# Seven-product units whose second half is added by accumulating transfers, in a hybrid encoder layer on one core

## The chip, the core and the metric

The kernel runs on one core of a Trainium2 chip. Time is what the device takes for one execution, in microseconds (us). A core has TensorE (matmuls; PE in the profile, PEld for its weight loads), VectorE (DVE), ScalarE (ACT), GpSimd (POOL) and SyncE (SP, which here only issues transfers), each with its own queue of instructions that it runs in order. Matmuls write to PSUM, eight banks of 128 x 512 float32; all else is in SBUF or in the chip's main memory (HBM).

## What is computed

One layer is applied to two sequences, a sample of 1024 positions and a prompt of 512, with shared weights and 2048 features:

```python
h = rms_norm(x, norm_g)
z = h @ w_in                     # 2048 x 5632
c_val, c_glu, c_gate, q, k, v, a_gate = jnp.split(z, split_points, axis=-1)
...
conv_out = conformer_conv(c_val, c_glu, w_dw, b_dw, ln_g, ln_b, w_pw) * jax.nn.silu(c_gate)
attn_out = banded_sink_attention(q, k, v, sink) * jax.nn.silu(a_gate)
mix = jnp.concatenate([conv_out, attn_out], axis=-1) @ w_out
return x + mix
```

`conformer_conv` is `c_val * sigmoid(c_glu)`, a convolution of 31 taps in each channel, a layer norm, a silu and a product with `w_pw`. The attention is banded and has rotary positions on q and k. A final RMS norm follows. Everything is float32: each operand is split into a high and a low part, and a product is three matmuls (high-high, high-low, low-high).

## The kernel before

**Units.** The input projection of the sample is done by 44 units (`Unit`). A unit takes two blocks of 128 columns of `w_in`, half of the depth (1024 features, called g = 0 or 1) and all 1024 positions. It sees this as a product of 2 x 2 blocks, and makes it with seven block products instead of eight: `make0` to `make3` (L120 to L150) form the sums of weights on VectorE and split them into parts, `block_sums` (L549) does the like with the tokens. Each product is 4 x 3 = 12 matmuls of 512 columns (L179). The products go to three accumulating banks; after each, `tap` takes the bank's content into one of four results, named (0,0), (0,1), (1,1), (1,0) by half of the positions and column block. Results are complete after products 1, 4, 5 and 6, counted from 0.

**Four stages.** 8 convolution units at g = 0, the same 8 at g = 1, 14 others (gates, keys and values, queries) at g = 1, the same 14 at g = 0. So there are two kinds. A *half-depth* unit (the first and third stage) copies or adds its products into new tiles (`tap_part`: ScalarE copies at L213 for products 0, 2, 3, 6; VectorE adds at L220 for the rest) and stores the four results to HBM (`part`). A *finishing* unit (second and fourth stage) loads these four tiles back (`load_parts`, L159 to L164, on SyncE's queue), either when it opens or already after product 4 of the unit ahead of it, adds all seven products to them on VectorE (`tap_sum`, L205) and calls `done` on each complete result. In the second and fourth stage the first two units run side by side.

**What `done` does.** For a convolution unit (`gated`, L673): the gate's column is scaled (L681), goes through a sigmoid (L682) and is scaled again (L683); once both columns of one half are there, they are multiplied (L687) and stored. For the fourteen others: a query's or key's result is turned (`rope`, L748 to L751, on VectorE), a gate's or value's result is scaled (L696) and then goes through a silu (L701, ScalarE) or is transposed (`turn_value`).

**Tiles.** The results lie in tiles from `E()`, which hands out tiles of two pools of four by turns; silu, rope, and other code take tiles from the same pools. Prepared weights (`hl`) have three buffers, raw ones three.

**What sets the order.** The program is written down once, in Python, and a scheduler places each engine's instructions by priority and by when they can run, using estimates of its own. `urgently` and `high_priority(URGENT)` move code ahead by 400 places: weight preparation and `tap`, with `done` in it, are written so. Three lanes (`attn`, `conv`, `prep`) hold work that is fed in between: for each three matmuls `tick` credits a lane 3 x 216 = 648, times its rate, and a lane's work pays what it yields. The convolution taps (`taps`, L720) of the sample go through the `conv` lane. The mean squares (`rms_ahead`, L616 to L630) and then the scaling of the prompt's input (`scale_ahead`, L639 to L653) go through the `prep` lane at rate 1; the first ends with a reciprocal root (`rsqrt`, L486 to L491) and a yield, the second begins with `spread` (L493 to L506), which puts the 512 numbers on all partitions: small VectorE instructions (L498, L499, L504) and two matmuls with ones (L505), in whose result the scaling is done (L651).

**Signs.** The sums are written as additions only. One token sum (`s1`) and one of the two columns come out negative; the sign is taken back in `val`, in the taps' weights, in the silu's scale and in `turn_value`.

After the sample's units follow the prompt's projections and the products with `w_pw` and `w_out` as plain jobs (L439), attention among them, and a last pass (L1165).

Of the kernel before, what the change touches and what calls it, by code (L numbers as in the profile page):

```python
# [46 lines left out]

SUMS = ("A11", "A12", "S2", "s1", "S3", "S4", "A22")
BANK = (0, 1, 0, 2, 0, 2, 0)
# [32 lines left out]
class Unit:  # L82
# [37 lines left out]
    def make0(self):  # L120
# [6 lines left out]
        return t  # L127

    def make1(self):
        add = lambda o, x, y: self.e.nc.vector.tensor_tensor(o, x, y, ALU.add)  # L130
        self.t = self.raw()
        add(self.t[:, 0], self.r1[:, 0], self.r2[:, 0])
        add(self.t[:, 1], self.t[:, 0], self.r2[:, 1])
        t = self.e.hl_tile()
        self.e.parts(t[:, 0], t[:, 1], self.t)
        return t

    def make2(self):
        self.e.nc.vector.tensor_tensor(self.r2[:, 0], self.r2[:, 0], self.r2[:, 1], ALU.add)
        t = self.e.hl_tile()  # L140
        self.e.parts(t[:, 0], t[:, 1], self.r2)
        self.r2 = None
        return t

    def make3(self):
        self.e.nc.vector.tensor_tensor(self.r1[:, 1], self.r1[:, 1], self.t[:, 1], ALU.add)
# [51 lines left out]
    def tap(self, step):  # L198
        if self.done:
            self.tap_sum(step)  # L200
        else:
            self.tap_part(step)

    def tap_sum(self, step):
        add = lambda n, b: self.e.nc.vector.tensor_tensor(self.d[n], self.bank[b], self.d[n], ALU.add)  # L205
        n = ((0, 0), (0, 0), (0, 1), (1, 1), (1, 1), (0, 1), (1, 0))[step]
        add(n, (0, 1, 0, 2, 0, 2, 0)[step])
        if step in (1, 4, 5, 6):
            self.done(n[0], n[1], self.d.pop(n))

    def tap_part(self, step):
        e, nc = self.e, self.e.nc
        copy = lambda n, b: nc.scalar.activation(self.d[n], self.bank[b], AF.Copy)  # L213
        n = ((0, 0), (0, 0), (0, 1), (1, 1), (1, 1), (0, 1), (1, 0))[step]
        b = (0, 1, 0, 2, 0, 2, 0)[step]
        if step in (0, 2, 3, 6):
            self.d[n] = e.E()
            copy(n, b)
        else:
            nc.vector.tensor_tensor(self.d[n], self.bank[b], self.d[n], ALU.add)  # L220
        if step in (1, 4, 5, 6):
            e.store(self.part[n[0]][n[1]], self.d.pop(n))

# [34 lines left out]
class Encoder:  # L258
# [84 lines left out]
    def constants(self):  # L343
        nc, a = self.nc, self.a

        def load(key, shape):
            t = self.const.tile([P] + shape, F32, name="c_" + key)
            nc.sync.dma_start(t, a[key])
            return t

        self.norm_g = load("norm_g", [ND])
        self.norm_n = self.const.tile([P, ND], F32, name="norm_n")
        nc.vector.tensor_scalar(self.norm_n, self.norm_g, -1.0, None, ALU.mult)
        self.ones = self.const.tile([P, P], F32, name="ones")
        nc.vector.memset(self.ones, 1.0)
        self.ones_r = self.const.tile([P, P], F32R, name="ones_r")
        nc.vector.tensor_copy(self.ones_r, self.ones)

        def rest():
            self.ident = load("ident", [P])  # L360
            self.mask = load("mask", [3 * P])

            self.w_dw = load("w_dw", [NC, TAPS])
            nc.vector.tensor_scalar(self.w_dw, self.w_dw, -1.0, None, ALU.mult)
# [44 lines left out]
    def run(self, items):  # L409
# [3 lines left out]
        for n, item in enumerate(items):  # L413
# [3 lines left out]
            if isinstance(item[0], Unit):  # L417
                ahead = items[n + 1]
# [90 lines left out]
class Sequence:  # L509


    def __init__(self, e, s):
# [19 lines left out]
        if s == 1:  # L532
            self.xr_d = dram("xr_d", [2, self.T], ND // 2)
        else:
            self.h_d = dram("h_d", [self.T], NC)
            self.sums_d = {(g, n): dram(f"sum_{g}_{n}", [W], HALF) for g in (0, 1) for n in ("s1", "S2", "S3", "S4")}

# [11 lines left out]
    def block_sums(self, k0, k1, x0, x1):  # L549
# [8 lines left out]
        return {"s1": s1, "S2": s2, "S4": t, "S3": s3}  # L558

# [14 lines left out]
    def first_sums(self, x):  # L574
# [5 lines left out]
        for j in range(HALF):  # L580
            sums = self.block_sums(j, j + HALF, x[j], x[j + HALF])
            for name in ("S2", "s1", "S3", "S4"):
                self.token_sum(name, 0, j, sums[name])
                e.store(self.sums_d[0, name][j], sums[name])
# [16 lines left out]
    def load_sum(self, name, g):  # L601
        e = self.e
        out = []
        for j in range(HALF):
            x = e.PT("p", NP, [W])
            if name in ("s1", "S2", "S3", "S4"):
                src = self.sums_d[g, name][j]
# [8 lines left out]
    def rms_ahead(self):  # L616
# [12 lines left out]
        e.rsqrt(self.rcol, v, self.B)  # L629
        yield 500  # L630

# [65 lines left out]

    def silu_of(self, dst, sign):
# [64 lines left out]
    def value(self, g, accs):  # L763
        e = self.e
        z = e.G()
        e.nc.scalar.activation(z, accs[0], AF.Copy)
        e.prep.add(self.turn_value(g, 0, z, 1.0))

    def negative_value(self, g):
        def done(t, z):  # L770
            self.scaled(z, t)
            self.e.attn.add(self.turn_value(g, t, z, -1.0))

        return done

    def turn_value(self, g, c, z, sign):
# [5 lines left out]
        nc.scalar.activation(z, ps, AF.Copy, scale=sign)  # L782
        e.store(self.v_d[g][:, c * W : c * W + W], z)
# [96 lines left out]
    def units(self):  # L880

        e, w = self.e, self.e.a["w_in"]

        def both(cols, name, done):
# [8 lines left out]
        for i in range(0, NC, 2):  # L893
            done = each(self.silu_of(self.gate_d[i], 1.0), self.silu_of(self.gate_d[i + 1], -1.0))
            gates.append(both((GATE + i, GATE + i + 1), f"gate{i}", done))
        rest = gates[:2] + [
            both((K + g, V + g), f"kv{g}", each(self.rotate(self.k_d[g]), self.negative_value(g))) for g in range(2)
        ]
        for h in range(HEADS):
            turn = self.rotate(self.q_d[h // GROUP][:, h % GROUP])  # L900
            rest.append(both((Q + h, AG + h), f"q{h}", each(turn, self.silu_of(self.ag_d[h], -1.0))))
        return conv, rest + gates[2:]

    def jobs(self):
        e, w = self.e, self.e.a["w_in"]
        job = lambda c, evac, **kw: Job(w[c], list(range(ND)), self.T, self.rhs, evac, **kw)
        conv = lambda i: [
# [497 lines left out]
```

## Time and profile before

| | |
|---|---|
| median of 3 runs | 2232.35 us (2229.7 to 2236.6) |
| the profiled execution | 2230.47 us |
| its span in the profile | 2228.7 us |
| mean granted TensorE clock | 0.984 |
| the first, second, third and fourth stage of units | about 0 to 188, to 346, to 634, to 937 us |
| transfers issued by GpSimd | none |

A row of the timeline gives start, length, engine, line and operation, what is written and read by the program's names, how many were merged, and in brackets how long the engine stood idle before and what ended that. A row of the waits reads "who <- for whom: us in total, times, longest". In a row for stretches of time each engine's busy time stands with its instruction count, then the granted TensorE clock, the share of the DMA engines and GB/s.

These are the chain that ended last, by engine, and the whole span in 40 slices, in tenths of each slice:

```profile
PE 68%; DVE 17%; DMA 9%; issue 4%; ACT 3%; SPq 0%; ACTq 0%; DVEq 0%
```

```profile
PE   6999998899989999999999999999999999999998
DVE  8648999999999999999677879977673578446343
```

The chain runs through TensorE for two thirds; VectorE is at nine tenths or more from the fourth slice to the eighteenth, which are the second to the fourth stage.

### The profile page before, as it was taken

What the parts mean: (1) busy time and instruction counts of PE and PEld (TensorE: products, weight loads), DVE (VectorE), ACT (ScalarE), POOL (GpSimd) and SP (SyncE); (2) the same over time, 40 slices, a digit from 0 to 9 for tenths busy, and PEclk for the clock granted to TensorE, in tenths of its full rate; (3) what the DMA queues carried; (4) which work ended last, traced back from release to release, by engine and by line L of the source; (5) the groups of instructions that cost most, each with busy time, mean ns of one, the idle gap of its engine ahead of it and who ended that gap; (6) DMA issues with size and microseconds to landing.
All of it is one profiled execution on the core that took longest, in us unless ns stands there. A gap on an engine that the chain in (4) does not pass through costs nothing.

```text
span 2228.7 us, 26104 instructions
## 1 busy us (share of the span) xinstructions
PE 2144.1 (96%) x9510; PEld 1754.4 (79%) x9510; DVE 1732.5 (78%) x2608; ACT 927.5 (42%) x1400; POOL 0.2 (0%) x4
## 2 busy tenths in 40 slices
PE   6999998899989999999999999999999999999998
PEld 4877786688867887788888888887888778888886
DVE  8648999999999999999677879977673578446343
ACT  5455324233343222433345446654562446322232
POOL 0000000000000000000000000000000000000000
PEclk8999999899999999999999999999999999999999
DMA  8866644633365545733333533337543466527342
GB/s 285 308 202 224 216 128 165 217 129 128 132 232 170 165 142 179 242 127 121 125 113 110 168 106 117 109 119 251 170 151 109 137 213 209 171 102 264 95 133 76
DMA packets 195072, 365.48 MB, mean 164 GB/s; under 512 B 17536, under 2 KB 75264, under 8 KB 194944
## 3 DMA queue, kind: packets, MB, share of 16 engines
q1 hardware_dynamic: 194944, 363.82, 49.0%
q8 instruction: 74, 1.21, 0.2%
q14 instruction: 54, 0.44, 0.1%
HBM read 276.72 MB, written 87.03 MB: 163 GB/s over the span
## 4 chain that ended last, share of the span: by engine, by line
PE 68%; DVE 17%; DMA 9%; issue 4%; ACT 3%; SPq 0%; ACTq 0%; DVEq 0%
PE a L439 18%; PE a L179 10%; PE b L439 9%; PE c L439 9%; PE c L179 5%; DVE hl L333 3%; DVE f L720 3%; PE s L830 2%; PE b L179 2%; PE a L1165 2%; PE s L1165 2%; DMA u<-q_d 2%; PE pv L862 2%; DMA raw<-w_in 1%; PE pt L867 1%
## 5 line engine op out<-in xcount | busy, mean ns | idle before, releaser
L332 ACT ACTIVATE hl<-raw 128x1024 fp32r<-128x1024 f32 (+1 forms) x367 | 369.7, 1008 | 651.7 <-PE a L439 138.4
L333 DVE TENSOR_TENSOR hl<-raw,hl 128x1024 fp32r<-128x1024 f32 (+1 forms) x367 | 424.5, 1157 | 206.6 <-ACT hl L332 200.9
L179 PE MATMUL a<-t,hl 128*128 128x512 f32 x1968 | 487.4, 399 | 29.3 <-ACT t L335 8.5
L439 PE MATMUL a<-t,hl 128*128 128x512 f32 x2112 | 506.1, 391 | 0.0
L179 PEld LDWEIGHTS a<-t,hl 128*128 128x128 f32 x1968 | 376.7, 193 | 119.8 <-ACT t L335 8.9
L439 PEld LDWEIGHTS a<-t,hl 128*128 128x128 f32 x2112 | 393.3, 188 | 79.1
L720 DVE SCALAR_TENSOR_TENSOR f<-f,c_w_dw,f 128x1024 f32<-128x1024 f32 (+1 forms) x464 | 452.7, 1010 | 2.5 <-ACT f L715 2.4
L439 PE MATMUL b<-t,hl 128*128 128x512 f32 x1056 | 255.8, 393 | 4.4 <-ACT hl L332 2.5
L179 PE MATMUL c<-t,hl 128*128 128x512 f32 x984 | 243.8, 393 | 12.5 <-ACT t L332 7.7
L439 PE MATMUL c<-t,hl 128*128 128x512 f32 x1056 | 253.7, 392 | 0.0
L439 PEld LDWEIGHTS b<-t,hl 128*128 128x128 f32 x1056 | 196.3, 188 | 44.2 <-ACT hl L332 3.2
L179 PEld LDWEIGHTS c<-t,hl 128*128 128x128 f32 x984 | 185.7, 189 | 55.3 <-ACT t L332 9.4
L439 PEld LDWEIGHTS c<-t,hl 128*128 128x128 f32 x1056 | 197.0, 188 | 39.8
L179 PE MATMUL b<-t,hl 128*128 128x512 f32 x492 | 119.0, 389 | 0.0
L179 PEld LDWEIGHTS b<-t,hl 128*128 128x128 f32 x492 | 92.4, 188 | 19.2
L1165 PE MATMUL a<-hl,t 128*128 128x512 f32 x192 | 74.7, 390 | 0.0
L332 ACT ACTIVATE a<-pt 128x512 fp32r<-128x512 f32 x64 | 38.1, 595 | 86.4 <-PE pt L867 86.1
L830 PE MATMUL s<-t,a 128*128 128x384 f32 (+1 forms) x288 | 58.6, 329 | 9.9 <-ACT a L332 9.0
L130 DVE TENSOR_TENSOR raw<-raw,raw 128x512 f32<-128x512 f32 x82 | 56.1, 684 | 14.6 <-DMA raw<-w_in 12.3
L844 ACT ACTIVATE p<-p,tiny 128x384 f32<-128x384 f32 (+1 forms) x96 | 54.5, 570 | 29.3 <-DVE tiny L841 29.1
L333 DVE TENSOR_TENSOR a<-pt,a 128x512 fp32r<-128x512 f32 x64 | 44.0, 687 | 29.1 <-ACT a L332 28.9
L830 PEld LDWEIGHTS s<-t,a 128*128 128x128 f32 x288 | 47.8, 188 | 20.7 <-ACT a L332 13.2
(245 smaller groups left out, 2049.9 us busy)
## 6 DMA issues: line engine op xcount, KB each, us to landing
raw<-w_in SPq DMA_DIRECT2D x169, 512.0 KB, 4.0
raw<-w_out SPq DMA_DIRECT2D x64, 512.0 KB, 3.7
raw<-w_out SPq DMA_DIRECT2D x64, 256.0 KB, 3.3
raw<-w_pw SPq DMA_DIRECT2D x24, 512.0 KB, 3.6
f<-xT_s SPq DMA_DIRECT2D x38, 256.0 KB, 6.1
f<-x_s SPq DMA_DIRECT2D x16, 512.0 KB, 7.2
f<-x_p SPq DMA_DIRECT2D x13, 512.0 KB, 6.9
p<-xT_s SPq DMA_DIRECT2D x24, 256.0 KB, 3.6
```

The source lines that it names most:

```text
L130: add = lambda o, x, y: self.e.nc.vector.tensor_tensor(o, x, y, ALU.add)
L179: nc.tensor.matmul(acc, hl[:, l, o, j, :], toks[j][:, r], start=step in FRESH and j == 0 and q == 0, stop=step in LAST and j == HALF - 1 a ...
L332: nc.scalar.activation(hi, x, AF.Copy)
L333: nc.vector.tensor_tensor(lo, x, hi.bitcast(F32), ALU.subtract)
L439: nc.tensor.matmul(job.acc[0], hl[:, l, kk // HALF, kk % HALF, :], r, start=i == 0 and p == 0, stop=i == nk - 1 and p == 2,)
L720: nc.vector.scalar_tensor_tensor(t, h[:, j : j + T], w(j), t, ALU.mult, ALU.add)
L830: nc.tensor.matmul(ps[:, 0:n], qs[:, x, h], k[y][:, keys], start=p == 0, stop=p == 2)
L844: nc.scalar.activation(p[:, 0:n], p[:, 0:n], AF.Exp, bias=nm[:, h : h + 1], accum_out=l[:, h : h + 1])
L862: nc.tensor.matmul(pv, v[x][:, vs], pt[:, y], start=i == 0 and p == 0, stop=i == last and p == 2)
L867: nc.tensor.transpose(tp[:, h], p[:, i * P : (i + 1) * P], e.ident)
L1165: nc.tensor.matmul(acc, self.mix[self.KS[i]][:, m, b * P : (b + 1) * P], part[l].rearrange("p a b -> p (a b)"), start=i == 0 and p == 0, s ...
```

## The change

It has three parts. First, a finishing unit no longer loads its partial sums ahead. Both kinds of unit tap alike: products 0, 2, 3 and 6 are copied on ScalarE, 1, 4 and 5 added on VectorE. When a result is complete, a half-depth unit stores it; a finishing unit has a transfer issued by GpSimd that reads the stored partial sum and adds it into the result's tile, and calls `done` on that tile right behind. Second, weights and tokens are summed with differences where additions were, so that no result is negative and the sign flips go. Third, `rms_ahead` ends with a yield of 15000 instead of 500.

```diff
 def make1(self):
-    add(self.t[:, 0], self.r1[:, 0], self.r2[:, 0])
-    add(self.t[:, 1], self.t[:, 0], self.r2[:, 1])
+    self.sub(self.t[:, 0], self.r2[:, 0], self.r1[:, 0])
+    self.sub(self.t[:, 1], self.r2[:, 1], self.t[:, 0])
...
-def load_parts(self):
-    if self.done and not self.d:
-        for n in ((0, 0), (0, 1), (1, 1), (1, 0)):
-            self.d[n] = self.e.E()
-            self.e.nc.sync.dma_start(self.d[n], self.part[n[0]][n[1]])
...
 def tap(self, step):
+    e, nc = self.e, self.e.nc
     n = ((0, 0), (0, 0), (0, 1), (1, 1), (1, 1), (0, 1), (1, 0))[step]
+    bank = self.bank[BANK[step]]
     if step in (0, 2, 3, 6):
         self.d[n] = e.E()
+        nc.scalar.activation(self.d[n], bank, AF.Copy)
     else:
+        nc.vector.tensor_tensor(self.d[n], bank, self.d[n], ALU.add)
     if step in (1, 4, 5, 6):
+        part, d = self.part[n[0]][n[1]], self.d.pop(n)
+        if self.done:
+            e.add_into(d, part)
+            self.done(n[0], n[1], d)
+        else:
+            e.store(part, d)
...
+def add_into(self, dst, src):
+    self.nc.gpsimd.dma_start(dst, src, accum_op=ALU.add)
...
 def run(self, items):
-                    u.load_parts()
-                    if step == 4 and isinstance(ahead[0], Unit) and len(ahead) == 1:
-                        ahead[0].load_parts()
...
 def block_sums(self, k0, k1, x0, x1):
-    nc.vector.scalar_tensor_tensor(s1, x0[:, W:], col(e.norm_n, k0), t, ALU.mult, ALU.add)
-    nc.vector.scalar_tensor_tensor(s2, x0[:, :W], col(e.norm_n, k0), s1, ALU.mult, ALU.subtract)
-    nc.vector.scalar_tensor_tensor(t, x1[:, :W], col(e.norm_n, k1), s2, ALU.mult, ALU.subtract)
+    nc.vector.scalar_tensor_tensor(s1, x0[:, W:], col(e.norm_g, k0), t, ALU.mult, ALU.add)
+    nc.vector.scalar_tensor_tensor(s2, x0[:, :W], col(e.norm_n, k0), s1, ALU.mult, ALU.add)
+    nc.vector.scalar_tensor_tensor(t, x1[:, :W], col(e.norm_g, k1), s2, ALU.mult, ALU.subtract)
...
 def rms_ahead(self):
-    yield 500
+    yield 15000
...
 def val(self, i, accs):
-    nc.vector.scalar_tensor_tensor(h[:, PAD : PAD + self.T], accs[0], -1.0, self.sig, ALU.mult, ALU.mult)
+    nc.vector.tensor_tensor(h[:, PAD : PAD + self.T], accs[0], self.sig, ALU.mult)
...
 def silu_of(self, dst):
-        self.e.nc.scalar.activation(z, z, AF.Silu, scale=sign)
+        self.e.nc.scalar.activation(z, z, AF.Silu)
```

`make2` and `make3` change as `make1` does; the taps' weights are no longer multiplied by -1, and `turn_value` has no sign.

More of the change, by code (lines that the diff above doesn't have):

```diff
@@ L45 @@
 HALF = 4
-SUMS = ("A11", "A12", "S2", "s1", "S3", "S4", "A22")
+SUMS = ("A11", "A12", "S2", "S1", "S3", "S4", "A22")
 BANK = (0, 1, 0, 2, 0, 2, 0)
@@ L127, in make0, with sub @@
         return t
+    def sub(self, out, x, y):
+        self.e.nc.vector.tensor_tensor(out, x, y, ALU.subtract)
     def make1(self):
-        add = lambda o, x, y: self.e.nc.vector.tensor_tensor(o, x, y, ALU.add)
         self.t = self.raw()
-        add(self.t[:, 0], self.r1[:, 0], self.r2[:, 0])
-        add(self.t[:, 1], self.t[:, 0], self.r2[:, 1])
+        self.sub(self.t[:, 0], self.r2[:, 0], self.r1[:, 0])
+        self.sub(self.t[:, 1], self.r2[:, 1], self.t[:, 0])
         t = self.e.hl_tile()
@@ L138, in make2 @@
     def make2(self):
-        self.e.nc.vector.tensor_tensor(self.r2[:, 0], self.r2[:, 0], self.r2[:, 1], ALU.add)
+        self.sub(self.r2[:, 0], self.r2[:, 1], self.r2[:, 0])
         t = self.e.hl_tile()
@@ L145, in make3 @@
     def make3(self):
-        self.e.nc.vector.tensor_tensor(self.r1[:, 1], self.r1[:, 1], self.t[:, 1], ALU.add)
+        self.sub(self.r1[:, 1], self.r1[:, 1], self.t[:, 1])
         t = self.e.hl_tile()
@@ L363, in rest @@
             self.w_dw = load("w_dw", [NC, TAPS])
-            nc.vector.tensor_scalar(self.w_dw, self.w_dw, -1.0, None, ALU.mult)
             self.b_dw = load("b_dw", [NC])
@@ L417, in run @@
             if isinstance(item[0], Unit):
-                ahead = items[n + 1]
                 for u in item:
                     u.open()
-                    u.load_parts()
                 for step in range(7):
@@ L535, in __init__ @@
             self.h_d = dram("h_d", [self.T], NC)
-            self.sums_d = {(g, n): dram(f"sum_{g}_{n}", [W], HALF) for g in (0, 1) for n in ("s1", "S2", "S3", "S4")}
+            self.sums_d = {(g, n): dram(f"sum_{g}_{n}", [W], HALF) for g in (0, 1) for n in ("S1", "S2", "S3", "S4")}
     def rhs(self, k):
@@ L581, in first_sums @@
             sums = self.block_sums(j, j + HALF, x[j], x[j + HALF])
-            for name in ("S2", "s1", "S3", "S4"):
+            for name in ("S2", "S1", "S3", "S4"):
                 self.token_sum(name, 0, j, sums[name])
@@ L605, in load_sum @@
             x = e.PT("p", NP, [W])
-            if name in ("s1", "S2", "S3", "S4"):
+            if name in ("S1", "S2", "S3", "S4"):
                 src = self.sums_d[g, name][j]
@@ L696, in scaled, with silu_of @@
         self.e.nc.vector.tensor_tensor(z, z, self.R[:, t * W : t * W + W], ALU.mult)
-    def silu_of(self, dst, sign):
+    def silu_of(self, dst):
         def done(t, z):
             self.scaled(z, t)
-            self.e.nc.scalar.activation(z, z, AF.Silu, scale=sign)
+            self.e.nc.scalar.activation(z, z, AF.Silu)
             self.e.store(dst[:, t * W : t * W + W], z)
@@ L766, in value, with value_of, turn_value @@
         e.nc.scalar.activation(z, accs[0], AF.Copy)
-        e.prep.add(self.turn_value(g, 0, z, 1.0))
-    def negative_value(self, g):
+        e.prep.add(self.turn_value(g, 0, z))
+    def value_of(self, g):
         def done(t, z):
             self.scaled(z, t)
-            self.e.attn.add(self.turn_value(g, t, z, -1.0))
+            self.e.attn.add(self.turn_value(g, t, z))
         return done
-    def turn_value(self, g, c, z, sign):
+    def turn_value(self, g, c, z):
         e, nc = self.e, self.e.nc
@@ L781, in turn_value @@
             nc.tensor.transpose(ps[:, j * P : (j + 1) * P], z[:, j * P : (j + 1) * P], e.ident)
-        nc.scalar.activation(z, ps, AF.Copy, scale=sign)
+        nc.scalar.activation(z, ps, AF.Copy)
         e.store(self.v_d[g][:, c * W : c * W + W], z)
@@ L893, in units @@
         for i in range(0, NC, 2):
-            done = each(self.silu_of(self.gate_d[i], 1.0), self.silu_of(self.gate_d[i + 1], -1.0))
+            done = each(self.silu_of(self.gate_d[i]), self.silu_of(self.gate_d[i + 1]))
             gates.append(both((GATE + i, GATE + i + 1), f"gate{i}", done))
         rest = gates[:2] + [
-            both((K + g, V + g), f"kv{g}", each(self.rotate(self.k_d[g]), self.negative_value(g))) for g in range(2)
+            both((K + g, V + g), f"kv{g}", each(self.rotate(self.k_d[g]), self.value_of(g))) for g in range(2)
         ]
@@ L900, in units @@
             turn = self.rotate(self.q_d[h // GROUP][:, h % GROUP])
-            rest.append(both((Q + h, AG + h), f"q{h}", each(turn, self.silu_of(self.ag_d[h], -1.0))))
+            rest.append(both((Q + h, AG + h), f"q{h}", each(turn, self.silu_of(self.ag_d[h]))))
         return conv, rest + gates[2:]
@@ L905, in jobs @@
         e, w = self.e, self.e.a["w_in"]
-        job = lambda c, evac, **kw: Job(w[c], list(range(ND)), self.T, self.rhs, evac, **kw)
+        job = lambda c, evac: Job(w[c], list(range(ND)), self.T, self.rhs, evac)
         conv = lambda i: [
```

19 lines of the change are left out of this document (1 added, 18 removed).

## The prediction

> **What bounds the kernel now.** I read the page's head first, then the stages (busy time by stretches), then the waits, and last the order of the work inside one stage.
>
> ```profile
> span 2228.7 us, 26104 instructions
> PE 2144.1 (96%) x9510; PEld 1754.4 (79%) x9510; DVE 1732.5 (78%) x2608; ACT 927.5 (42%) x1400; POOL 0.2 (0%) x4
> ```
>
> TensorE is busy for 96% of the span. A busy TensorE can still be slow, so I take its undisturbed pace from the timeline:
>
> ```profile
> 193.83 2.88 PE L179 MATMUL b<-t,hl 128*128 128x512 f32 x12
> 196.55 2.88 PE L179 MATMUL s<-t,hl 128*128 128x512 f32 x12
> ```
>
> One product of 12 matmuls starts 2.72 us after the one before, so a unit of seven products needs 19.04 us. Against this floor I hold the stages that the change touches (stretch, its length, then busy time of each engine):
>
> ```profile
> core 0: us, PE busy (x) PEld busy (x) DVE busy (x) ACT busy (x) POOL busy (x), PEclk, DMA share, GB/s
> 188.00:346.00 158.00, 154.91 (x675) 127.17 (x674) 149.77 (x206) 56.98 (x74) 0.00 (x0) 0.99 0.53 174
> 346.00:634.00 288.00, 271.32 (x1179) 222.66 (x1178) 281.69 (x327) 102.33 (x137) 0.00 (x0) 0.97 0.47 162
> 634.00:690.50 56.50, 45.85 (x171) 34.70 (x170) 53.66 (x73) 29.05 (x41) 0.00 (x0) 0.88 0.68 225
> 690.50:890.70 200.20, 195.53 (x857) 158.10 (x856) 198.01 (x273) 53.64 (x64) 0.00 (x0) 1.00 0.50 164
> 890.70:937.00 46.30, 41.94 (x172) 33.40 (x171) 43.70 (x60) 22.30 (x33) 0.00 (x0) 0.93 0.73 244
> ```
>
> The rows are: eight finishing convolution units, fourteen half-depth units, then the fourteen finishing units cut into 2, 10 and 2. Time over the floor: 158.0 - 8 x 19.04 = 5.7 us; 288.0 - 14 x 19.04 = 21.4 us; 56.5 - 38.1 = 18.4 us; 200.2 - 190.4 = 9.8 us; 46.3 - 38.1 = 8.2 us. That is all there is to win in these stages. VectorE is full in every one of them (198.0 of 200.2 us in the ten units), so here it, not TensorE, decides what is lost. The largest single loss stands in the waits and in the two timelines:
>
> ```profile
> PE s L505 <- DVE u L504: 16.7, 2, 14.6
> 381.66 2.43 PE L179 MATMUL b<-t,hl 128*128 128x512 f32 x10
> 398.67 1.58 PE L505 MATMUL s<-u,ones_r 128*128 128x512 f32 x2 [14.58 <-DVE u L504]
> 385.20 0.16 DVE L626 TENSOR_TENSOR tiny<-sq 128x4 f32<-128x4 f32 x1 [0.63 <-ACT f L623]
> 395.14 0.15 DVE L491 TENSOR_TENSOR stat<-tiny,tiny 128x4 f32<-128x4 f32 x1
> 396.41 0.16 DVE L498 CAST tinyr<-stat 128x4 fp32r<-128x4 f32 x1
> 398.53 0.87 DVE L504 TENSOR_SCALAR u<-c_ident,tiny 128x128 fp32r<-128x128 f32 x4
> ```
>
> TensorE stands for 14.6 us in front of one spread of the second sequence: the spread's matmul is in its queue, and VectorE has the chain from the sums (L626) through the root (L491) to the diagonals (L504) still ahead of it, at 1.2 to 1.3 us a link because a convolution tap lies between any two. This is 14.6 of the 21.4 us.
>
> **The change, part by part.**
>
> *The spread.* After the root the lane now yields 15000 instead of 500. The lane earns 648 for each three matmuls, so 23 such steps pass, 69 matmuls, 69 x 2.72/12 = 15.6 us of products ahead of the spread. The chain ends 399.4 - 384.1 = 15.3 us after TensorE arrives now, so all of the 14.6 us could go. But while TensorE runs, VectorE also has its products' work. The taps' line alone, in the 288 us stage:
>
> ```profile
> 346.00:634.00 288.00, 153.10 (x122) 0.97 0.47 162
> ```
>
> Without them a unit costs VectorE (281.7 - 153.1)/14 = 9.2 us, so up to 9.2 x 15.6/19.04 = 7.5 us may come ahead of the chain. Left over: 0 to 7.5 us; I take 3, under the middle, because the root's part of the chain can be done before. Gain **11.6 us**, ends 7 and 14.6.
>
> *The adds that go.* Now a finishing unit adds each of its seven products into a loaded partial sum on VectorE. From now on products 0, 2, 3 and 6 are copied by ScalarE, and three are added.
>
> ```profile
> 188.00:346.00 158.00, 37.47 (x55) 0.99 0.53 174
> 634.00:937.00 303.00, 65.32 (x96) 0.97 0.57 188
> 855.81 0.69 DVE L750 TENSOR_TENSOR g<-g,f 128x512 f32<-128x512 f32 x1
> 856.42 0.68 DVE L205 TENSOR_TENSOR u<-a,u 128x512 f32<-128x512 f32 x1
> 857.02 0.68 DVE L751 TENSOR_TENSOR g<-g,u 128x512 f32<-128x512 f32 x1
> L213 ACT ACTIVATE u<-a 128x512 f32<-128x512 f32 x40 | 23.8, 594 | 59.9 <-PE a L179 52.4 <-DVE g L687 4.2 <-DMA gate_d<-u 3.3
> ```
>
> The first two rows are those of the add's line alone (55 and 96; 154 in all, seven for each of 22 units). An add lasts 0.68 us but starts overlap, and one takes 0.60 us of the queue. 22 x 4 = 88 adds go: **52.8 us of VectorE**, 2.4 us a unit. ScalarE gets 88 x 0.594 = 52 us; it is busy for 57 of 158 us and 105 of 303 us there, so the copies are hidden, and in the half-depth units the same copies release the same banks without loss (its idle time before them ended with the product itself). If VectorE's waits held ScalarE too, the copies would come late, and the banks with them; that is in the slower rival.
>
> *The transfers.* 88 loads of 256 KB leave SyncE, which issued them up to a unit early. 88 accumulating transfers come onto GpSimd's queue, each issued only when its sum is complete. They read the same bytes, and GpSimd has nothing else to do. What is new is a wait: the finishing code follows the transfer at once, and its first VectorE instruction needs it landed. In the fourteen units that is all four results (L696, L748), in the eight convolution units three (the fourth waits for its partner anyway): 14 x 4 + 8 x 3 = **80 waits**. Behind each on VectorE stand the low parts of the next weights (L333), the weight sums and the adds that empty banks; TensorE waits for all of these. The trace shows no accumulating transfer, so I bound its uncovered wait. Nearest are plain transfers of that size:
>
> ```profile
> DMA to landing us min/median/max: 2.4/3.3/6.5
> u<-q_d SPq DMA_DIRECT2D x24, 256.0 KB, 4.3
> ACT a L332 <- DMA u<-q_d: 14.7, 10, 3.8
> u<-ag_d SPq DMA_DIRECT2D x24, 256.0 KB, 3.7
> DVE u L989 <- DMA u<-ag_d: 23.2, 16, 3.1
> 845.68 0.68 DVE L205 TENSOR_TENSOR u<-a,u 128x512 f32<-128x512 f32 x1
> 846.28 0.68 DVE L130 TENSOR_TENSOR raw<-raw,raw 128x512 f32<-128x512 f32 x1
> 846.88 0.68 DVE L696 TENSOR_TENSOR u<-u,f 128x512 f32<-128x512 f32 x1
> ```
>
> The first row is the landing of the partial sums' loads now. Where a consumer is queued right behind a load, as here, the wait left over is 14.7/24 = 0.61 us for the queries and 23.2/24 = 0.97 us for the gates, though landing takes 4.3 and 3.7 us: other work stands in front. The last three rows show why: between the add and the first finishing instruction the order has put other ready work. So the ends are 0 (covered) and 3.3 us (nothing in between), with more if accumulating is slower than reading. I take 0.6 us, the queries' row, because these consumers also have a raised priority. 80 x 0.6 = 48 us. Of the 52.8 us that VectorE saved, **5 us** remain; TensorE feels part of it, as VectorE fills what comes free with taps. I take 2 us.
>
> *The rest at nothing.* Sums become differences with as many instructions of the same shape, and the sign flips ride in instructions that stay; one small multiplication at the start and a scale in 8 instructions go. SyncE's 88 issues leave, which lets its other loads go earlier; no row shows TensorE waiting for SyncE in these stages, so this is nothing, or at most the 3.3 us of one load.
>
> Sum: 2230.5 (the profiled execution: the span and 1.8 us around it) - 11.6 - 2 = **2217 us**, 0.6% under it; the median of the runs shown, 2232.35, lies 1.9 us above that execution.
>
> By the Trainium skill (DMA: Bandwidth & Descriptors, "Anatomy of one DMA — SWDGE (gpsimd) path") a transfer issued from GpSimd takes 2.0 us plus its bytes over 436 GB/s; my estimate from it is 2.6 us, under the 3.3 us of the loads above, and by it the sum would be the first rival's 2206. The same page ("Latency and other measured facts") speaks against the change: the first byte comes after about 1 us from GpSimd and 0.6 us from SyncE; with that 0.4 us on each wait the sum would be an estimate of 2217 + 80 x 0.4 = 2249. No run here shows either yet.
>
> **The rivals.**
>
> *All covered.* If VectorE's other work always outlasts the transfer, the 52.8 us are its own. Then the 9.8 and 5.7 us go, but for the unit ends, and a little of the 18.4: 11 us more than in my sum, **2206 us**. For it: VectorE is never idle in these stages, so something is always ready. Against it: the two rows of waits above.
>
> *Slower: VectorE held at the finishing code.* One mechanism: the first instruction behind each accumulating transfer stops VectorE's queue. It costs 80 w for an uncovered wait of w us, and wins 52.8 + 11.6 = 64.4 us; it decides from w = 0.8 us. At w = 1.5 us the price is 120 us, and the time 2230.5 + 55.6 = **2286 us**. For it: VectorE has no slack in these stages (2.2 us in 200), an add to a tile must read it besides the source, and the issue now comes last instead of early. Against it: 0.61 us in the queries' row.
>
> *The spread's wait moves.* VectorE's backlog is as long 15.6 us later, and TensorE stops there instead: 2230.5 - 2 = **2228 us**, no change. For it: the taps between the links remain, and the matmul still follows its diagonals at once. Against it: the root would be done by then.
>
> **How the numbers follow.** My sum 0.38, all covered 0.12, the spread moved 0.13, slower 0.37. The first two are faster by more than 0.3%, which is about what a measurement of this kernel tells from no change: 0.50. Same 0.13, slower 0.37. The range goes from 2199, under the covered case with the spread's whole 14.6 us and SyncE's 3.3 us, up to the slower rival at 1.5 us; waits beyond that, perhaps a third of that rival, are left out: 2199 to 2286.
>
> **What would show it.** The spread: its wait under 7.5 us. The adds: 66 left, and 88 more copies. The waits: the finishing lines' idle time ended by the accumulating transfers; under 64 us in total if I am right, over 64 us with units well above 20 us each if the slower rival is. The ten units at 19.0 to 19.3 us would show all covered. I am wrong if accumulating transfers land much later than the plain loads' 3.3 us, or if the order leaves them less in front than it left those.

## The result and the profile after

The changed kernel takes **2338.66 us** (median of 4 runs, 2332.48 to 2345.73); the kernel before took 2231.02 us beside it (4 runs). The ratio is **1.048, 95% interval 1.0435 to 1.0524**: slower by 4.8%, above the predicted range. The profiled execution took 2344.41 us.

These are the head of the page of the changed kernel, and its engines in 40 slices:

```profile
span 2342.6 us, 26174 instructions
PE 2185.0 (93%) x9510; PEld 1779.5 (76%) x9510; DVE 1685.2 (72%) x2519; ACT 969.4 (41%) x1488; POOL 77.0 (3%) x92
```

```profile
DVE  8657778999996777779657887987675377636243
...
POOL 0001111000001111110000000000000000000000
```

VectorE has 89 instructions fewer (the 88 adds and one small multiplication) and is busy for 47.3 us less; ScalarE has its 88 copies more. The work that was to go did go. But VectorE, at nine tenths from the fifth slice to the nineteenth before (counted from one), is now at six to eight wherever GpSimd issues. The stages, cut at the same places of the program as in the prediction:

```profile
189.00:380.00 191.00, 165.31 (x677) 133.00 (x676) 144.19 (x186) 75.42 (x110) 26.41 (x31) 0.93 0.61 155
380.00:657.00 277.00, 270.48 (x1178) 222.20 (x1177) 263.27 (x309) 98.44 (x134) 1.58 (x2) 0.99 0.46 156
657.00:725.80 68.80, 46.23 (x170) 33.66 (x169) 59.16 (x75) 31.48 (x47) 5.27 (x6) 0.88 0.65 191
725.80:983.40 257.60, 217.16 (x858) 173.32 (x858) 195.99 (x250) 73.54 (x104) 35.63 (x41) 0.89 0.52 126
983.40:1038.00 54.60, 44.07 (x179) 34.64 (x178) 41.03 (x53) 25.52 (x39) 7.01 (x8) 0.94 0.71 198
```

Against before: the eight finishing convolution units +33.0 us, the fourteen half-depth units -11.0, then +12.3, the ten units **+57.4**, the last two +8.3. Of the 113.9 us of span, 100.0 arise between the start of the second stage and the end of the fourth, all of them in finishing units. The 11.0 us and the 12.3 right behind are the spread's stop, which moves: TensorE no longer stands at the spread, and stands 11.7 us at the change of stage (a single stop there took 4.8 us before; spread_alone below shows it by itself). (12.9 us more arise after the units and 1 before; their cause stays open.) In the ten units VectorE is idle for 257.6 - 196.0 = 61.6 us, where it was idle for 2.2. The waits of VectorE inside that stretch name the cause:

```profile
DVE u L732 <- DMA g<-part_q: 26.0, 15, 3.6
DVE u L732 <- DMA g<-part_kv: 10.5, 4, 4.0
DVE u L680 <- DMA u<-part_q: 8.9, 8, 1.6
DVE g L680 <- DMA g<-part_q: 5.4, 5, 1.6
DVE u L680 <- DMA u<-part_kv: 3.7, 2, 2.2
DVE u L680 <- DMA u<-part_gate: 2.9, 1, 2.9
DVE g L680 <- DMA g<-part_gate: 2.2, 1, 2.2
```

L732 is the first line of `rope`, L680 the scaling, both the first VectorE instruction of the finishing code; each releaser is an accumulating transfer. With one more of 0.4 us they sum to 60.0 of the 61.6 us. Over the whole kernel, the groups of instructions show the same (the number after the bar is busy time, then comes the idle time just before and what ended it):

```profile
L732 DVE TENSOR_TENSOR u<-g,f 64x512 f32<-64x512 f32 x20 | 13.7, 687 | 39.8 <-DMA g<-part_q 29.3 <-DMA g<-part_kv 10.5
L680 DVE TENSOR_TENSOR u<-u,f 128x512 f32<-128x512 f32 x18 | 12.5, 692 | 23.7 <-DMA u<-part_gate 11.0 <-DMA u<-part_q 8.9 <-DMA u<-part_kv 3.7
L680 DVE TENSOR_TENSOR g<-g,f 128x512 f32<-128x512 f32 x18 | 12.4, 691 | 25.4 <-DMA g<-part_gate 19.6 <-DMA g<-part_q 5.4 <-DMA g<-part_kv 0.4
L665 DVE TENSOR_TENSOR g<-g,f 128x512 f32<-128x512 f32 x8 | 5.5, 693 | 17.8 <-DMA g<-part_conv 17.8
```

With three groups of the convolution units that are not shown here (L665 and L671, 22.3 us) that is **129 us in 71 waits**, 1.8 us each. One unit's timeline shows what a wait is made of, VectorE first and then GpSimd:

```profile
877.62 0.68 DVE L201 TENSOR_TENSOR u<-a,u 128x512 f32<-128x512 f32 x1
878.23 0.68 DVE L130 TENSOR_TENSOR raw<-raw,raw 128x512 f32<-128x512 f32 x1
878.83 1.28 DVE L704 SCALAR_TENSOR_TENSOR f<-f,c_w_dw,f 128x1024 f32<-128x1024 f32 x1
880.02 0.68 DVE L201 TENSOR_TENSOR g<-c,g 128x512 f32<-128x512 f32 x1
880.62 1.21 DVE L323 TENSOR_TENSOR hl<-raw,hl 128x1024 fp32r<-128x1024 f32 x1
882.52 0.69 DVE L680 TENSOR_TENSOR u<-u,f 128x512 f32<-128x512 f32 x1 [0.69 <-DMA u<-part_q]
883.13 1.28 DVE L704 SCALAR_TENSOR_TENSOR f<-f,c_w_dw,f 128x1024 f32<-128x1024 f32 x1
885.97 0.69 DVE L680 TENSOR_TENSOR g<-g,f 128x512 f32<-128x512 f32 x1 [1.56 <-DMA g<-part_q]
```

```profile
878.72 0.87 POOL L313 DMA_DIRECT2D u<-part_q  x1 [8.94 <-DVE u L201]
881.11 0.86 POOL L313 DMA_DIRECT2D g<-part_q  x1 [1.52 <-DVE g L201]
```

The sum in u is complete at 878.30; its transfer is issued at 878.72 and its result used at 882.52, 4.2 us after the sum. In between the order has put work up to 881.83: 3.5 us of **cover**. 0.7 us stay open. For g the sum ends at 880.70 and the cover at 884.41, 3.7 us later, and the result is used at 885.97. This unit is no exception: matched transfer by transfer in the trace, the 88 have a median cover of 3.6 us, and landing minus cover, summed where it is positive, gives 127 us. TensorE stands too, since the add that empties bank a is behind these waits. In the ten units it stops ten times, once in each, for 35.4 us in all. The waits of TensorE there, and four of the stops in its timeline:

```profile
PE a L174 <- DVE u L201: 35.4, 10, 5.5
```

```profile
804.49 8.05 PE L174 MATMUL a<-t,hl 128*128 128x512 f32 x24 [5.37 <-DVE u L201]
852.94 7.37 PE L174 MATMUL a<-t,hl 128*128 128x512 f32 x24 [2.82 <-DVE u L201]
878.37 8.62 PE L174 MATMUL a<-t,hl 128*128 128x512 f32 x24 [4.46 <-DVE u L201]
902.74 5.76 PE L174 MATMUL a<-t,hl 128*128 128x512 f32 x24 [2.16 <-DVE u L201]
```

There is more in these rows' second column: 24 matmuls take 5.6 us at the undisturbed pace; after a stop of 2.16 us they take 5.76, after 2.82 us 7.37, after 4.46 us 8.62, after 5.37 us 8.05. The granted clock over these four rows is 0.69, 0.77, 0.64 and 1.00 in turn, and 0.89 over the whole stretch (1.00 before); TensorE's busy time grows from 195.5 to 217.2 us there. The stops and the 21.6 us of slower matmuls make 57.0 of the 57.4 us. They are the same time as VectorE's 60.0 us of waits, seen from TensorE, and not a cost beside it.

### The profile page after: what moved, and what is told of

The parts are those of the page before. It is cut to its first block, busy times and chain, and to the rows that moved or that the text cites. A ratio compares the mean times of both kernels' runs of the same rounds, so it can differ in the third digit from the quotient of the medians.

```text
span 2342.6 us, 26174 instructions
## 1 busy us (share of the span) xinstructions
PE 2185.0 (93%) x9510; PEld 1779.5 (76%) x9510; DVE 1685.2 (72%) x2519; ACT 969.4 (41%) x1488; POOL 77.0 (3%) x92
## 4 chain that ended last, share of the span: by engine, by line
PE 51%; issue 16%; DMA 4%; DVE 2%; POOL 2%; ACT 1%; SPq 0%; POOLq 0%; ACTq 0%; DVEq 0%
PE a L423 18%; PE b L423 9%; PE c L423 9%; PE s L814 2%; PE a L1148 2%; PE s L1148 2%; PE pv L846 2%; PE a L174 2%; DMA u<-q_d 1%; DMA u<-ag_d 1%; POOL g L313 1%; PE pt L851 1%; PE pv L1148 1%; PE b L1148 1%; PE c L1148 1%
## 5 line engine op out<-in xcount | busy, mean ns | idle before, releaser
L174 PE MATMUL a<-t,hl 128*128 128x512 f32 x1968 | 507.2, 411 | 84.5 <-DVE u L201 35.4
L174 PEld LDWEIGHTS a<-t,hl 128*128 128x128 f32 x1968 | 389.8, 200 | 182.6 <-DVE u L201 39.6
L423 PE MATMUL a<-t,hl 128*128 128x512 f32 x2112 | 507.1, 392 | 0.0
L423 PEld LDWEIGHTS a<-t,hl 128*128 128x128 f32 x2112 | 393.9, 188 | 79.6
L174 PE MATMUL c<-t,hl 128*128 128x512 f32 x984 | 251.6, 404 | 31.4 <-ACT g L199 21.9
L423 PE MATMUL b<-t,hl 128*128 128x512 f32 x1056 | 260.4, 399 | 9.1 <-DVE hl L323 7.1
L423 PE MATMUL c<-t,hl 128*128 128x512 f32 x1056 | 253.6, 392 | 0.0
L174 PE MATMUL b<-t,hl 128*128 128x512 f32 x492 | 119.7, 390 | 0.2 <-DVE t L326 0.2
L130 DVE TENSOR_TENSOR raw<-raw,raw 128x512 f32<-128x512 f32 x123 | 84.4, 686 | 18.3 <-DMA raw<-w_in 15.2
L199 ACT ACTIVATE g<-a 128x512 f32<-128x512 f32 x67 | 39.7, 592 | 92.0 <-PE a L174 91.6
L814 PE MATMUL s<-t,a 128*128 128x384 f32 (+1 forms) x288 | 59.2, 332 | 12.6 <-ACT a L322 11.6
L323 DVE TENSOR_TENSOR a<-pt,a 128x512 fp32r<-128x512 f32 x64 | 44.0, 688 | 35.4 <-ACT a L322 35.1
```

Source lines behind the costliest of these rows:

```text
L130: self.e.nc.vector.tensor_tensor(out, x, y, ALU.subtract)
L174: nc.tensor.matmul(acc, hl[:, l, o, j, :], toks[j][:, r], start=step in FRESH and j == 0 and q == 0, stop=step in LAST and j == HALF - 1 a ...
L199: nc.scalar.activation(self.d[n], bank, AF.Copy)
L323: nc.vector.tensor_tensor(lo, x, hi.bitcast(F32), ALU.subtract)
L423: nc.tensor.matmul(job.acc[0], hl[:, l, kk // HALF, kk % HALF, :], r, start=i == 0 and p == 0, stop=i == nk - 1 and p == 2,)
L814: nc.tensor.matmul(ps[:, 0:n], qs[:, x, h], k[y][:, keys], start=p == 0, stop=p == 2)
```

## The experiments

**My theory after the result:** the cost is the wait that the order leaves uncovered, landing minus cover, paid by VectorE which had no idle time; nothing else in the change costs. **Rivals:** the difference form or the later spread costs; VectorE's adds were worth little, so that any wait shows; accumulating costs by itself through GpSimd's queue, covered or not; the copies on ScalarE come late. Ratios are to the kernel before on the same chip, with 95% intervals. The "waits" are VectorE's idle time ended by transfers of partial sums; "above" is a kernel's ratio less that of the kernel without these transfers, times 2231 us.

| kernel | median us | ratio | waits us | above us |
|---|---|---|---|---|
| spread_alone | 2233.81 | 0.9991 (0.9978 to 1.0005) | | |
| loads_ahead | 2237.09 | 1.0005 (0.9995 to 1.0014) | 0.0 | |
| no_add | 2210.95 | 0.9889 (0.9874 to 0.9904) | none | 0 |
| plain_sync | 2227.94 | 0.9960 (0.9945 to 0.9975) | 12.1 | 16 |
| plain_pool | 2271.19 | 1.0155 (1.0135 to 1.0174) | 58.0 | 59 |
| later2 | 2282.61 | 1.0205 (1.0190 to 1.0220) | 54.4 | 71 |
| later4 | 2292.45 | 1.0252 (1.0228 to 1.0276) | 66.3 | 81 |
| the change | 2338.66 | 1.0480 (1.0435 to 1.0524) | 129.0 | 132 |
| spread_rate | 2228.24 | 0.9959 (0.9945 to 0.9973) | | |
| rate_alone | 2234.79 | 0.9991 (0.9975 to 1.0006) | | |
| early_one | 2229.19 | 0.9969 (0.9952 to 0.9987) | 0.0 | |
| early_rate | **2223.02** | **0.9943 (0.9925 to 0.9961)** | 2.1 | |

**The parts one by one.** The later spread alone, in the kernel before:

```diff
-        yield 500
+        yield 15000
```

> The kernel before with the yield of 15000 alone. Theory of the prediction: the 14.6 us wait of TensorE at the prompt's spread shrinks to 0 to 7.5 us, time 2216 to 2224 us (ratio 0.993 to 0.997). Rival, the wait only moves: ratio 0.999 to 1.001 and a wait over 10 us elsewhere.

No difference that can be measured, though the stop at the spread shrank. The waits of TensorE, for the kernel before (its row of the spread, 14.6 us, stands in the prediction) and then for this one:

```profile
PE a L179 <- DVE t L336: 7.0, 2, 4.8
```

```profile
PE a L179 <- DVE t L336: 16.6, 2, 14.4
...
PE s L505 <- DVE u L504: 7.5, 2, 5.2
```

The longest stop at the spread fell by 9.4 us, from 14.6 to 5.2; the longest one for the low parts of the tokens at the change of stage (about 640 us) grew by 9.6, from 4.8 to 14.4. The stretch between the two points, in the same kernel:

```profile
409.00:640.00 231.00, 216.64 (x941) 178.45 (x942) 226.86 (x255) 79.09 (x103) 0.00 (x0) 0.97 0.48 160
```

VectorE, the third busy time, is full for 226.9 of 231.0 us. A shorter stop of TensorE gives it no time for its work, and the two engines meet again where TensorE needs VectorE's low parts. A stop moved, it was not removed.

The form and the spread with the partial sums loaded ahead as before (SyncE, seven VectorE adds):

```diff
+    def load_parts(self):
+        if self.done and not self.d:
+            for n in ((0, 0), (0, 1), (1, 1), (1, 0)):
+                self.d[n] = self.e.E()
+                self.e.nc.sync.dma_start(self.d[n], self.part[n[0]][n[1]])
...
-        if step in (0, 2, 3, 6):
+        if step in (0, 2, 3, 6) and not self.done:
```

> The changed kernel with the partial sums loaded ahead by SyncE again and all seven adds on VectorE: what is left of the change is the form of the sums and the yield. If the accumulating transfers are the whole loss: the time of the yield alone, 2216 to 2224 us. If the differences or the order that they lead to cost something: over 2235 us.

1.0005: the difference form and the later spread cost nothing that shows and bring nothing. (The time is over the 2235 us of the second case only because the kernel before took 2236.15 us beside it; the first case had still counted on a gain of the yield.) All 4.8% lie in the partial sums.

The change without its transfers, so that the first half's partial sums are left out of the results:

```diff
-                e.add_into(d, part)
```

> The changed kernel without the accumulating transfers: the finishing code takes the second half's sums alone, so the addition of the first half is left out of the output. Copies on ScalarE stay. Theory (VectorE held for 129 us in front of the finishing code): the whole loss goes, 2190 to 2212 us, under the yield alone by what the 88 adds taken from VectorE are worth. Rival (the copies on ScalarE come late and hold the banks): most of the loss stays, over 2290 us.

0.9889. Beside loads_ahead that is 26 us for 52.8 us of adds taken off VectorE (and the loads, which nothing waited for): the relief is real and larger than I had priced it. Late copies on ScalarE by themselves are ruled out, since this kernel has them. The transfers and their waits cost 132 us against this.

**Which transfer costs what.** The transfer at its place, as a plain load, from GpSimd and then from SyncE. It overwrites the sum, so the second half's sums are left out of the results; instructions and the waits that follow stay. The second line is that of plain_pool, the third that of plain_sync.

```diff
-        self.nc.gpsimd.dma_start(dst, src, accum_op=ALU.add)
+        self.nc.gpsimd.dma_start(dst, src)
...
+        self.nc.sync.dma_start(dst, src)
```

> The changed kernel with GpSimd's transfer as a plain load, without adding: it overwrites the result's tile with the partial sum, so the second half's sums are left out of the output. If the adding makes the transfer slow: landing falls from 4.5 us to about 3.3 us, and 80 waits times 1.2 us go, about 2245 us. If the place of the issue is the cost: landing over 4 us and 2320 us or more.

> The same plain load issued by SyncE at the same place, also without adding (the second half's sums are left out of the output). If GpSimd's 0.87 us of issue makes the difference: waits fall by about 0.5 to 0.9 us each, 2260 to 2300 us. If any transfer behind the complete sum holds VectorE: over 2300 us. SyncE now waits for the sums ahead of the weights' loads, which could add to it.

One row of the transfers' issues (median us from issue to landing is last) and one group of instructions, first the change's issues (its group stands above, with 39.8 us of idle time):

```profile
g<-part_q POOLq DMA_DIRECT2D x24, 256.0 KB, 4.6
```

plain_pool:

```profile
g<-part_q POOLq DMA_DIRECT2D x24, 256.0 KB, 3.1
```

```profile
L732 DVE TENSOR_TENSOR u<-g,f 64x512 f32<-64x512 f32 x20 | 13.7, 687 | 23.2 <-DMA g<-part_q 18.6 <-DMA g<-part_kv 4.4
```

plain_sync:

```profile
g<-part_q SPq DMA_DIRECT2D x24, 256.0 KB, 2.8
```

```profile
L732 DVE TENSOR_TENSOR u<-g,f 64x512 f32<-64x512 f32 x20 | 13.7, 687 | 1.7 <-DMA g<-part_q 1.3
```

The idle time before the same 20 instructions goes 39.8, 23.2, 1.7 us as the landing goes 4.6, 3.1, 2.8. Counted from the end of the sum instead of the issue, the medians over all 88 transfers are 4.9, 3.5 and 2.9 us, against a median cover of 3.6, 3.5 and 3.6 us. So the total is a steep function of the landing once that passes the cover, and "waits" and "above" in the table agree within 4 us for all three kinds of transfer. **Shown:** the loss is the uncovered wait. Of the 132 us, 73 come with the adding, 43 with GpSimd instead of SyncE, 16 with loading late at all. Both times missed what was expected: plain_pool's landing fell as its first case said, but its waits fell by 71 us instead of 96; plain_sync lies 32 us under its lower range, which counted the sooner issue and left out that nothing is added.

**More cover.** The finishing code is written two products later, and without the raised priority; in the second kernel four products.

```diff
-                self.done(n[0], n[1], d)
+                e.finish_later(lambda: self.done(n[0], n[1], d))
...
+    def finish_later(self, fn):
+        self.pending.append([LATER, fn])
```

> The changed kernel with the finishing code written two products (5.4 us) behind its transfer and without raised priority; the transfers are the same. Theory (only the missing cover costs): VectorE's idle time ended by these transfers falls from 129 us to under 25 us, time 2200 to 2225 us. Rival (the transfers themselves cost: GpSimd's 0.87 us each, their load on the DMA engines): over 2290 us with no long waits of VectorE.

> As later2, with the finishing code four products (10.9 us) behind its transfer. Theory (VectorE is held where a transfer has not landed, and ScalarE behind VectorE): 10.9 us is more than the longest landing seen (9.9 us), so waits under 10 us in total and a time near that without any adding, 2208 to 2222 us, faster than before. Rival (the two-product run already took what cover can give; the rest is a cost of the transfers or of the tiles held longer): 2265 to 2290 us.

later2 takes away over half of the loss of the change, and its waits fall from 129.0 to 54.4 us, where under 25 were expected; later4 should have ended them, and 66.3 us were left. Both expectations missed, so that part of my theory (write it later and it is covered) fell. The scheduler places an instruction by when it can run, not only by where it is written: transfer by transfer the median cover is 3.6 us in the change, about 6 in later2 and about 5.5 in later4, though the code is written 5.4 and 10.9 us later. Landing minus cover, summed where it is positive, gives 53 and 65 us, again nearly the waits of the table. later2's convolution stage shows what else remains, ScalarE and then TensorE:

```profile
292.54 0.63 ACT L683 ACTIVATE g<-g 128x512 f32<-128x512 f32 x1 [5.37 <-DVE g L682]
293.07 0.58 ACT L201 ACTIVATE g<-c 128x512 f32<-128x512 f32 x1
```

```profile
293.71 2.56 PE L175 MATMUL c<-t,hl 128*128 128x512 f32 x10 [3.04 <-ACT g L201]
```

L683 is the gate's sigmoid. It stands in ScalarE's queue waiting for VectorE's scaling (L682), and that is held 0.91 us by its transfer; the copy that empties bank c is behind it, and TensorE waits 3.04 us for that copy. So the wait reaches ScalarE as well. This fits later2 and later4 lying 15 to 17 us further above no_add than their waits, but no run separates it. That the waits did not shrink from two products to four is the cover that did not grow; why the scheduler left no more of it stays open.

**Cover from the other side.** Instead of finishing later, issue earlier: in loads_ahead, the result (0,1) is made of products 2 and 5. Its partial sum is accumulated right behind ScalarE's copy of product 2, 8.2 us before VectorE's add of product 5 needs the tile.

```diff
-            for n in ((0, 0), (0, 1), (1, 1), (1, 0)):
+            for n in ((0, 0), (1, 1), (1, 0)):
...
-        if step in (0, 2, 3, 6) and not self.done:
+        if step in (0, 2, 3, 6) and (not self.done or step == 2):
...
+            if self.done:
+                e.add_into(self.d[n], self.part[0][1])
```

> The kernel with loads ahead (2237.1 us beside a before of 2236.2), but the result (0,1) gets its partial sum by an accumulating transfer, issued behind ScalarE's copy of product 2; its VectorE add follows only after product 5, three products or 8.2 us later; the other three results keep their loads ahead and their adds. My theory (what costs is the wait that the order leaves uncovered, not the accumulating as such): 8.2 us is more than the 4.9 us that landing took behind a sum, so VectorE's idle time ended by these 22 transfers stays under 6 us in all, and the 22 adds that go are worth 25 x 22/88 = 6 us: 2228 to 2234 us, ratio 0.995 to 0.999. Rival (accumulating transfers cost by themselves, through GpSimd's queue or the tile that they hold, covered or not): at the changed kernel's 129/88 = 1.5 us each, 22 of them cost 32 us: 2255 us or more, ratio 1.01 or more.

0.9969, in favour of the theory and against the rival that accumulating costs by itself. The same transfers are as slow as in the change. VectorE takes these tiles up with the add of product 5, from bank c in most units. These are the adds from that bank; what idle time they have ends with the product, and none with a transfer:

```profile
g<-part_q POOLq DMA_DIRECT2D x8, 256.0 KB, 4.5
```

```profile
L209 DVE TENSOR_TENSOR u<-c,u 128x512 f32<-128x512 f32 x36 | 24.7, 686 | 4.2 <-PE c L180 4.2
L209 DVE TENSOR_TENSOR g<-c,g 128x512 f32<-128x512 f32 x25 | 17.2, 686 | 1.6 <-PE c L180 1.6
```

In one unit the copy ends at 778.90 us, the transfer lands at 783.8, and the add starts at 786.80. The 22 adds that go are worth 0.36% beside loads_ahead, 8 us; their share of the 26 us would be 6.5.

**The moved stop.** If VectorE's taps are what holds the spread and then the tokens, fewer taps should free both. The rate of the conv lane, with the later spread and then alone:

```diff
-RATES = (0.4, 0.9, 0.3, 1.0)
+RATES = (0.4, 0.8, 0.3, 1.0)
```

> The kernel before with the yield of 15000 and fewer taps in the third stage (0.8 for 0.9). In the run with the yield alone 9.4 us went at the spread and 9.5 us came at the change of stage, where TensorE waits for VectorE's token parts. Theory (VectorE is the one that is full, and a stop of TensorE gave it time for taps): with fewer taps the wait of 14.5 us at about 625 us falls under 8 us, 2221 to 2228 us. Rival (the wait at the change of stage has nothing to do with taps): it stays, 2232 to 2236 us.

> The kernel before with the taps' rate at 0.8 instead of 0.9 and the yield left at 500. Beside it stands the kernel with both edits, which took 2228.2 us against 2235.1. If the lower rate alone made that gain (fewer taps are put ahead of the work that TensorE waits for, wherever the stop stands): 2226 to 2230 us, with the stop ahead of the spread still over 8 us. Rival (the gain is that of the later spread, which the lower rate only kept from turning up again at the change of stage): 2233 to 2238 us, no change.

Together 0.9959; alone no change. The waits of TensorE, of the two in turn:

```profile
PE b L439 <- ACT t L335: 14.1, 1, 14.1
...
PE a L179 <- DVE t L333: 5.0, 1, 5.0
PE s L505 <- DVE u L504: 4.8, 2, 3.0
```

```profile
PE b L439 <- ACT t L335: 14.2, 1, 14.2
PE s L505 <- DVE u L504: 12.4, 2, 11.2
```

With both edits the spread and the change of stage are short, and the gain is 0.4%; with the rate alone the spread still stops TensorE for 11.2 us. Either edit alone only moves a stop. In both a new one of 14 us stands at the first of the plain jobs (L439), where ScalarE prepares tokens; what it would take to end that one stays open.

Last, the early transfer and the rate together:

> The kernel of the first run of this call (one result of four by an early accumulating transfer, three loaded ahead, yield 15000) with the taps' rate at 0.8. If covered accumulating transfers and the rate add up: 6 us and 7 us under the kernel before, 2221 to 2227 us, ratio 0.993 to 0.996, the shortest of all kernels that compute the whole layer. Rival (both only relieve VectorE, and the second relief finds nothing left to win): 2227 to 2231 us, ratio 0.996 to 0.998. If the early transfers cost by themselves: over 2245 us.

2223.02 us, 0.9943: of the kernels here that leave nothing out the lowest ratio. It is clearly shorter than early_one beside it (2229.19 us); against spread_rate, which ran on another chip, the intervals overlap, so that the early transfer adds to the rate is likely and not shown.

## Why the prediction was wrong

- **What bounds the kernel: right.** VectorE decides what is lost in these stages. 60.0 of its 61.6 idle us in the ten units are the new waits.
- **The spread: wrong in the sum.** 3 us were to be left of the stop, from 0 to 7.5; 5.2 were. But the step from a shorter stop to "Gain 11.6 us" failed: VectorE was full from there to the change of stage, and the stop turned up there (9.4 us less, 9.6 us more). The rival "The spread's wait moves" had the time right and the place wrong (not at the spread, but at the change of stage).
- **The adds that go: counts right, worth mis-sized.** 88 adds and 88 copies, as worked out. I priced their relief fully covered at 2 + 11 = 13 us; without any transfer the adds that go bring 26 us.
- **The transfers: the step that failed.** "I take 0.6 us" for each of 80 waits; there were 71 of 1.8 us, 129 us where I put 48. What was mis-sized is the landing: I bounded it by plain loads at 3.3 us, and an accumulating transfer took 4.1 to 5.3 by group. The plain transfer of plain_pool, which landed after 3.1 us, left 58 us, not far from my 48. My reason for the lower of two rows, "because these consumers also have a raised priority", did not bear on it: a priority that brings the consumer forward would shorten the cover, not lengthen it. No run changes the priority alone; later2 changes it together with the place. The mean of the waits lies between the ends of 0 and 3.3 us, the longest at 5.9 us beyond.
- **The balance of the two: failed as well.** I set the waits against the adds, 52.8 - 48 = 5 us. By the runs the adds are worth 26 us, and the waits cost their whole length; so even plain_pool, with 58 us of waits, is 1.55% slower than the kernel before.
- **The slower rival: its mechanism is what happened**, and its point of decision, 0.8 us, was passed. Its price of 120 us was close to the 129 us of waits; its credit of 64.4 us was not. By the runs: about -26 us for the adds, 0 for the spread and 132 for the transfers. That the price came so close is in part luck: it was 80 waits of a chosen 1.5 us, and there were 71 of 1.8.
- **The rest at nothing: right.** loads_ahead lies at 1.0005.
- **ScalarE's copies: right by themselves, late behind the wait.** The prediction had put that into the slower rival; later2's rows show it.
- **The two figures for a transfer from GpSimd.** By the Trainium skill, DMA: Bandwidth & Descriptors, "Anatomy of one DMA — SWDGE (gpsimd) path": my estimate from its fit was 2.6 us; it stands against 3.1 measured for a plain transfer from GpSimd and 4.6 for an accumulating one; by the measurement its result, the covered rival, was out of reach. The same page of the Trainium skill, "Latency and other measured facts", was the better warning: GpSimd's first byte comes 0.4 us later by it, and here the plain transfer from GpSimd landed 0.6 us later behind its sum than that from SyncE (3.5 against 2.9).

## What to carry to other kernels

Price a transfer that is put between two instructions as landing minus cover, where the cover is the work that the order leaves between producer and consumer on the waiting engine; read both from the timeline, and do not take code that is written later for code that runs later. Work taken off a full engine is worth about half of its length here, and a wait given to it costs its whole length, so an accumulating transfer pays only where its result is not needed for longer than it lands (8.2 us of cover was free; 3.6 us left 129 us of waits over 88 transfers). A stop of TensorE that a full engine causes is paid again at the next place where the two meet, unless that engine gets less to do before it.

## What the runs showed of the hardware

**Adding costs landing time.** In the group of 24 shown above, 256 KB from GpSimd's queue land 4.6 us after the issue when added and 3.1 us when copied; over all 88 it is 4.5 and 3.1. The issue itself is longer too, in the change and then in plain_pool (shortest, median, longest ns):

```profile
L313 POOL DMA_DIRECT2D g<-part_q x24: 862/865/888, 793.9 to 985.2; - x24
```

```profile
L313 POOL DMA_DIRECT2D g<-part_q x24: 536/536/552, 748.6 to 921.3; - x24
```

**A stop of TensorE can cost more than its length.** In the four rows above 2.16 us cost nothing further, 2.82 us another 1.8, 4.46 us another 3.0 and 5.37 us another 2.4. The Trainium skill (TensorE: Matmul & The Clock Gate, "Part 1: The HAM clock gate") says that the clock halves after an idle window of about 3.4 us, on windows that run freely, and returns after a busy one; the rows agree in kind, with a granted clock of 0.69, 0.77 and 0.64 behind the three longer stops and 1.00 behind the shortest, and show the fall already after a stop of 2.82 us.
